# Latent attention in uniform 1024-column steps over three rotating PSUM pairs

## Chip, cores, metric

One Trainium2 chip, all 8 cores, one launch. The time is device microseconds of the slowest core. Such a program has a second, slower state in some executions, in which the cores of a die show a lower granted clock (the share of full TensorE speed that the profile records); those runs are marked slow and only fast runs are compared.

## The reference, cut to what matters

```python
# 8 heads, rank-compressed q and kv; block-causal over 64-frame chunks
q  = (rms_norm(c_q,  g_q)  @ w_uq ).reshape(B, S, 8, 128 + 64)    # nope | rope
kv = (rms_norm(c_kv, g_kv) @ w_ukv).reshape(B, S, 8, 128 + 128)   # k_nope | v
s = (einsum('bqhd,bkhd->bhqk', q_nope, k_nope) + einsum('bqhd,bkd->bhqk', q_pe, k_pe)) * scale
p = softmax(where(k_chunk <= q_chunk, s, NEG))
y_mla = einsum('bhqk,bkhd->bqhd', p, v) * silu(z_mla)
# ... sliding-window and memory groups, output projection, residual, final norm
```

Each core owns 1024 queries of one batch and sees all 4096 keys. The mask is a part of the rotary operand (64 extra rows), so it needs no instruction of its own.

## The kernel before: the parts concerned

Scores stand transposed, keys on partitions and queries on columns. PSUM has 8 banks: 0 to 3 are two pairs for scores, 4 and 5 the outputs of the two query halves, 6 the softmax sums, 7 the single bank in which the next head's operands (Q, rotary Q, K, V) are built. DVE takes its instructions in program order: the prediction shows a cast that starts at 580.10 behind two adds, although its matmuls were done before 578.9.

```python
def rec_s(n):                       # one step: two key tiles, 512 - c0 queries
    ... 4 score matmuls into pair n % 2
    act(AF.Exp, pb[:, :, c0:512], DB[k][:, c0:512], ...)
    if pr == 1:                     # add four tiles to one, for the sums
        tt(ALU.add, q2, pa, pb);  tt(ALU.add, q4, q2[:, 0], q2[:, 1])

def rec_pv(n):
    ... 2 PV matmuls into bank 4 + half
    if pr == 1:
        matmul(bank 6, lhsT=ones, rhs=q4)            # inline sum
        if last:                                     # close a half
            act(AF.Ln, rim, bank 6); act(AF.Exp, rim, rim, scale=-1.0)
            tt(ALU.mult, tmm, bank 4 + half, rim);  tt(ALU.mult, gate, tmm, gate)

for n in range(len(steps)):         # 24 steps per head, widths 512 / 384 / 256 / 128
    rec_s(n)
    if n >= 2: rec_pv(n - 2)
    if gen_next: gen_next.pop(0)()  # one of 20 operand jobs, 512 columns, always in bank 7
```

A job is its matmuls and one evacuation, the copy from PSUM to SBUF: K by an ACT copy, V and Q by a DVE cast, rotary Q by two DVE multiplies and an add.

The softmax here doesn't subtract the row's maximum and nothing guards it: scores larger than these inputs give would overflow.

Of the kernel before, what the change touches and what calls it, by code (L numbers as in the profile page):

```python
# [6 lines left out]
F32 = mybir.dt.float32  # L7
BF16 = mybir.dt.bfloat16
# [6 lines left out]
KB = 1024  # L15
# [151 lines left out]
def build():  # L167
# [33 lines left out]
    def pf(b, c0, c1, p0=0, p1=128):  # L201
        o = (b % 2) * 512
        return DB[b // 2][p0:p1, o + c0:o + c1]
# [4 lines left out]
    def tt(op, out, a, b, reads, writes, eng="dve"):  # L208
        P.op(eng, lambda e: e.tensor_tensor(out=out, in0=a, in1=b, op=op), reads=reads, writes=writes)  # L209
# [5 lines left out]
    def cp(eng, out, in_, reads, writes):  # L215
        if eng == "act":
            act(AF.Copy, out, in_, reads, writes)
        else:
            P.op(eng, lambda e: e.tensor_copy(out=out, in_=in_), reads=reads, writes=writes)  # L219
# [552 lines left out]
    Qn = [P.sb("Qn", [128, 1024], BF16, (26 + 2 * i) * KB) for i in range(2)]  # L772
    Qp = [P.sb("Qp", [128, 1024], BF16, (30 + 2 * i) * KB) for i in range(2)]
    csq = P.sb("csq", [128, 1024], F32, 98 * KB)
    tq = P.sb("tq", [64, 2, 512], F32, 102 * KB)
    pm4 = [P.sb("pm4", [128, 2, 512], BF16, (106 + 2 * i) * KB) for i in range(4)]
    p2 = [P.sb("p2", [128, 2, 512], BF16, (150 + 2 * i) * KB) for i in range(2)]
    p4 = [P.sb("p4", [128, 512], BF16, (154 + i) * KB) for i in range(2)]
    rim = P.sb("rim", [128, 512], F32, 156 * KB)
    tmm = P.sb("tmm", [128, 512], F32, 158 * KB)  # L780
    P.dma("sp", csq.t[:], csq_d[:, :], csq, writes=[csq])
    for i in range(2):
        P.dma("pool", Qp[i].t[64:128, :], gtm_d[:, :], Qp[i], writes=[Qp[i]])
# [3 lines left out]
        P.dma("pool", wo[i].t[:].rearrange("p a b -> p (a b)"), wo_d[i], wo[i], writes=[wo[i]])  # L787
    kpeT.w = kpeT.w + oh_ev

    def gen(h, banks):  # L790
        s = h % 2
        K_, V_, Qn_, Qp_ = Kb[s], Vb[s], Qn[s], Qp[s]
        ch = []

        def qn(half, gb):
            hs = slice(half * 512, (half + 1) * 512)

            def mm(e):
                for kc in range(4):
                    ins = e.matmul(pf(gb, 0, 512), lhsT=wuq.t[:, kc, h * 256:h * 256 + 128], rhs=cqT.t[:, kc, hs],  # L800
                                   start=(kc == 0), stop=(kc == 3))
                return ins
            P.op("pe", mm, reads=[wuq, cqT], writes=[PS[gb]])
            cp("dve", Qn_.t[:, hs], pf(gb, 0, 512), [PS[gb]], [Qn_])

        def qp(half, gb):
            hs = slice(half * 512, (half + 1) * 512)

            def mm(e):
                for kc in range(4):  # L810
                    ins = e.matmul(pf(gb, 0, 512), lhsT=wuq.t[:, kc, h * 256 + 128:h * 256 + 256], rhs=cqT.t[:, kc, hs],
                                   start=(kc == 0), stop=(kc == 3))
                return ins
            P.op("pe", mm, reads=[wuq, cqT], writes=[PS[gb]])
            tt(ALU.mult, tq.t[:, 0, :], pf(gb, 0, 512, 0, 64), csq.t[0:64, hs], [PS[gb], csq], [tq])
            tt(ALU.mult, tq.t[:, 1, :], pf(gb, 0, 512, 64, 128), csq.t[64:128, hs], [PS[gb], csq], [tq])
            tt(ALU.add, Qp_.t[0:64, hs], tq.t[:, 0, :], tq.t[:, 1, :], [tq], [Qp_])
            Qp_.w = Qp_.w + mask_ev[s]

        def kg(c8, gb):  # L820
            def mm(e):
                for kc in range(2):
                    ins = e.matmul(pf(gb, 0, 512), lhsT=wukv.t[:, kc, h * 256:h * 256 + 128],  # L823
                                   rhs=kvnT.t[:, kc, c8 * 512:(c8 + 1) * 512], start=(kc == 0), stop=(kc == 1))
                return ins
            P.op("pe", mm, reads=[wukv, kvnT], writes=[PS[gb]])
            cp("act", K_.t[:, c8 * 512:(c8 + 1) * 512], pf(gb, 0, 512), [PS[gb]], [K_])

        def vg(c8, gb):
            def mm(e):  # L830
                for t4 in range(4):
                    tl = c8 * 4 + t4
                    for kc in range(2):
                        ins = e.matmul(pf(gb, t4 * 128, (t4 + 1) * 128), lhsT=kvnT.t[:, kc, tl * 128:(tl + 1) * 128],  # L834
                                       rhs=wukv.t[:, kc, h * 256 + 128:h * 256 + 256], start=(kc == 0), stop=(kc == 1))
                return ins
            P.op("pe", mm, reads=[wukv, kvnT], writes=[PS[gb]])
            cp("dve", V_.t[:, c8 * 4:(c8 + 1) * 4, :].rearrange("p a b -> p (a b)"), pf(gb, 0, 512), [PS[gb]], [V_])

        for half in range(2):  # L840
            ch.append((qn, half))
            ch.append((qp, half))
        for c8 in range(8):
            ch.append((kg, c8))
            ch.append((vg, c8))
        return [(lambda f=f, a=a, gb=banks[i % len(banks)]: f(a, gb)) for i, (f, a) in enumerate(ch)]

    for c in gen(0, list(range(8))):
        c()


    steps = []
    for h in range(8):
        for half in range(2):
            kgs = list(range(4 * half + 4))
            for kg_ in kgs:
                c0 = max(0, kg_ - 4 * half) * 128
                for pr in range(2):
                    tiles = [kg_, 8 + kg_] if pr == 0 else [16 + 2 * kg_, 17 + 2 * kg_]
                    steps.append((h, half, kg_, c0, pr, tiles, kg_ == 0, kg_ == kgs[-1]))  # L860
    SKEW = 1
    pendq = []
    gen_next = []
    cur_h = -1

    def rec_s(n):
        h, half, kg_, c0, pr, tiles, first, last = steps[n]
        s, k, pb = h % 2, n % 2, pm4[n % 4]

        def mm(e):  # L870
            for t in range(2):
                kc = slice(tiles[t] * 128, (tiles[t] + 1) * 128)
                qs = slice(half * 512 + c0, half * 512 + 512)
                e.matmul(pf(2 * k + t, c0, 512), lhsT=Kb[s].t[:, kc], rhs=Qn[s].t[:, qs], start=True, stop=False)  # L874
                ins = e.matmul(pf(2 * k + t, c0, 512), lhsT=kpeT.t[:, kc], rhs=Qp[s].t[:, qs], start=False, stop=True)  # L875
            return ins
        P.op("pe", mm, reads=[Kb[s], Qn[s], Qp[s], kpeT], writes=[PS[2 * k], PS[2 * k + 1]])
        act(AF.Exp, pb.t[:, :, c0:512], DB[k][:, :].rearrange("p (a b) -> p a b", b=512)[:, :, c0:512],
            [PS[2 * k], PS[2 * k + 1]], [pb], scale=MLA_SCALE)
        if pr == 1:  # L880
            pa = pm4[(n - 1) % 4]
            q2, q4 = p2[(n // 2) % 2], p4[(n // 2) % 2]
            tt(ALU.add, q2.t[:, :, c0:512], pa.t[:, :, c0:512], pb.t[:, :, c0:512], [pa, pb], [q2])
            tt(ALU.add, q4.t[:, c0:512], q2.t[:, 0, c0:512], q2.t[:, 1, c0:512], [q2], [q4])

    def rec_pv(n):
        h, half, kg_, c0, pr, tiles, first, last = steps[n]
        s, pb = h % 2, pm4[n % 4]
        ob, lb = 4 + half, 6
        q4 = p4[(n // 2) % 2]  # L890

        def mm(e):
            for t in range(2):
                ins = e.matmul(pf(ob, c0, 512), lhsT=Vb[s].t[:, tiles[t], :], rhs=pb.t[:, t, c0:512],  # L894
                               start=(first and pr == 0 and t == 0), stop=(last and pr == 1 and t == 1))
            return ins
        P.op("pe", mm, reads=[Vb[s], pb], writes=[PS[ob]])
        if pr == 1:
            P.op("pe", lambda e: e.matmul(pf(lb, c0, 512), lhsT=ones.t[:], rhs=q4.t[:, c0:512], start=first, stop=last),
                 reads=[q4, ones], writes=[PS[lb]])  # L900
            if last:
                hs = slice(half * 512, (half + 1) * 512)
                act(AF.Ln, rim.t[:], pf(lb, 0, 512), [PS[lb]], [rim])
                act(AF.Exp, rim.t[:], rim.t[:], [rim], [rim], scale=-1.0)
                tt(ALU.mult, tmm.t[:], pf(ob, 0, 512), rim.t[:], [PS[ob], rim], [tmm])
                tt(ALU.mult, gate.t[:, h, hs], tmm.t[:], gate.t[:, h, hs], [tmm, gatep[h][half]], [gatep[h][half]])

    xo = [None] * 8

# [1 line left out]
        xo[i] = P.sb("xo", [128, D], F32, off * KB)  # L911
        P.dma("sp", xo[i].t[:], xo_d[i], xo[i], writes=[xo[i]])

    for n in range(len(steps)):
        h = steps[n][0]
        if h != cur_h:
            cur_h = h
            gen_next = gen(h + 1, [7]) if h < 7 else []
        rec_s(n)
        if n >= 2:  # L920
            rec_pv(n - 2)
        if gen_next:
            gen_next.pop(0)()
        if h == 7 and n % 24 == 3:
            for i, off in enumerate((34, 126)):
                wo.append(P.sb("wo", [128, 16, 512], BF16, off * KB))
                P.dma("pool", wo[2 + i].t[:].rearrange("p a b -> p (a b)"), wo_d[2 + i], wo[2 + i], writes=[wo[2 + i]])
            for i, off in enumerate((2, 10, 114, 142)):
                load_xo(i, off)
    rec_pv(len(steps) - 2)  # L930
    rec_pv(len(steps) - 1)


    gfin = P.sb("gfin", [128, D], F32, 198 * KB)
# [173 lines left out]
```

## Time and profile before

| | before |
|---|---|
| fast runs | 1003.8, 1004.4, 1004.8 us |
| slow run | 1108.7 us |
| until the first operand job (core 0) | 474.0 us |
| head 0's operands | 14.4 us |
| attention stage: first scores to first projection matmul | 389.2 us |
| output projection to the end | 125.5 us |
| a head with jobs / head 7 | 51.3 / 29.1 us |

The last five rows are cut from core 0's timeline; the first four of these add up to its span of 1003.1 us. Here and below the attention stage begins with the first rotary score matmul, 0.2 us after the very first score, where the prediction begins it (so it has 14.2 for head 0's operands). The lines that carry this are shown in the prediction. DVE of the kernel before, in order of time, around the 3.27 us hole:

```profile
543.84 0.69 DVE L209 TENSOR_TENSOR tmm_137<-psd,rim_136 128x512 f32<-128x512 f32 x1
544.63 0.69 DVE L209 TENSOR_TENSOR gate_103<-tmm_137,gate_103 128x512 bf16<-128x512 f32 x1
545.24 1.47 DVE L209 TENSOR_TENSOR tq_127<-psd,csq_126 64x512 f32<-64x512 f32 x2
```

The rotary evacuation (`tq`) that PE waits for until 546.86 stands behind the two multiplies that close the previous half (`tmm`, `gate`), and these need two ACT operations on the sums. Here the two were done by 543.74 and cost nothing more, because two adds held DVE from 542.63 to 543.85: in front of this cast stand both, adds and multiplies.

### The profile page before, as it was taken

The numbers are of one execution on the slowest core, as the hardware profiler recorded it, in microseconds if no ns is written. First come the engines' busy times: TensorE is split into PE (matmuls) and PEld (weight loads), VectorE is DVE, ScalarE is ACT, GpSimd is POOL, SyncE is SP. The second block draws the span as 40 slices with busy tenths as digits, with TensorE's granted clock in tenths as the row PEclk, the third lists the DMA queues.
The fourth block names the chain that finished last, engine by engine and source line by source line (L and its number), as shares of the span: only waits on it lengthen the run. The fifth ranks groups of instructions, "written<-read, shape, count | busy, mean of one in ns | idle before, by whom it ended". The sixth has DMA issues, their size and how long they took to land.

```text
span 1003.1 us, 12701 instructions; the slowest of 8 cores (987.9 to 1003.1 us)
## 1 busy us (share of the span) xinstructions
PE 811.1 (81%) x4461; PEld 394.0 (39%) x4540; DVE 520.4 (52%) x750; ACT 433.4 (43%) x593; POOL 16.3 (2%) x32
## 2 busy tenths in 40 slices
PE   0687987695999899899777777777777878999995
PEld 0244543243454333344433344443444434434442
DVE  0456654575665587677734444444444443424333
ACT  1336556311014467546354554545454536712221
POOL 2010000000000000000000000000000000000000
PEclk9889998899899999899999999999999989999998
DMA  9999538342563223876400000000000002991222
GB/s 171 233 170 171 98 52 150 156 163 89 205 257 127 85 103 108 157 200 140 81 1 1 1 1 1 2 0 1 1 1 1 2 1 66 211 289 64 85 85 84
DMA packets 18466, 95.55 MB, mean 95 GB/s; under 512 B 1826, under 2 KB 6050, under 8 KB 9380
## 3 DMA queue, kind: packets, MB, share of 16 engines
q0 software_dynamic: 7168, 30.15, 18.7%
q1 hardware_dynamic: 11236, 64.59, 18.2%
q8 instruction: 37, 0.61, 0.3%
q14 instruction: 25, 0.20, 0.1%
HBM read 116.49 MB, written 8.39 MB: 124 GB/s over the span
## 4 chain that ended last, share of the span: by engine, by line
PE 53%; DVE 15%; DMA 11%; ACT 11%; issue 9%; DVEq 0%; SPq 0%; ACTq 0%; POOL 0%; POOLq 0%
PE psd L562 14%; PE psd L947 10%; PE psd L327 9%; DMA wo_141<-wo 4%; PE psd L875 4%; PE psd L874 3%; PE psd L823 3%; ACT pm_87_129 L206 3%; DMA hown_57<-xu 2%; DVE tq_127 L209 2%; DMA wst_76<-wkv 2%; DMA stage_85<-wti 2%; DVE p_90_132 L209 2%; PE psd L894 2%; DVE Vb_121 L219 2%
## 5 line engine op out<-in xcount | busy, mean ns | idle before, releaser
L823 PE MATMUL psd<-kvnT_53,wukv_117 128*128 128x512 bf16 x120 | 36.6, 381 | 57.0 <-DVE Vb_121 L219 27.5
L209 DVE TENSOR_TENSOR p_90_132<-pm_86_128,pm_87_129 128x1024 bf16<-128x1024 bf16 (+1 forms) x48 | 29.0, 603 | 90.6 <-ACT pm_87_129 L206 90.4
L562 PE MATMUL psd<-hown_57,ring_86 128*128 128x512 bf16 x280 | 69.7, 408 | 6.1 <-DVE kmT_93 L209 4.8
L209 DVE TENSOR_TENSOR p_91_133<-pm_88_130,pm_89_131 128x768 bf16<-128x768 bf16 (+2 forms) x48 | 24.7, 514 | 84.8 <-ACT pm_89_131 L206 84.8
L206 ACT ACTIVATE pm_86_128<-psd 128x1024 bf16<-128x1024 f32 (+1 forms) x48 | 42.3, 882 | 59.7 <-PE psd L875 23.4
L562 PE MATMUL psd<-hown_57,ring_88 128*128 128x512 bf16 x281 | 63.8, 379 | 4.3 <-DVE zrt_113 L209 2.1
L875 PE MATMUL psd<-Qp_125,kpeT_54 128*128 128x512 bf16 (+3 forms) x192 | 61.5, 334 | 1.0 <-issue 0.4
L875 PE MATMUL psd<-Qp_124,kpeT_54 128*128 128x512 bf16 (+3 forms) x192 | 61.5, 334 | 1.0 <-issue 0.4
L874 PE MATMUL psd<-Qn_122,Kb_118 128*128 128x512 bf16 (+3 forms) x184 | 57.9, 329 | 0.7 <-ACT Kb_118 L206 0.7
L874 PE MATMUL psd<-Qn_123,Kb_119 128*128 128x512 bf16 (+3 forms) x184 | 57.8, 328 | 0.5 <-ACT pm_86_128 L206 0.4
L327 PE MATMUL psd<-hown_57,wkv_63 128*128 128x512 bf16 x125 | 34.6, 440 | 26.1 <-DMA hown_57<-xu 25.9
L206 ACT ACTIVATE pm_89_131<-psd 128x768 bf16<-128x768 f32 (+2 forms) x48 | 35.4, 738 | 39.6 <-PE psd L875 38.8
L562 PEld LDWEIGHTS psd<-hown_57,ring_86 128*128 128x128 bf16 x288 | 29.4, 104 | 44.8 <-issue 16.8
L206 ACT ACTIVATE pm_87_129<-psd 128x1024 bf16<-128x1024 f32 (+1 forms) x48 | 42.3, 881 | 10.0 <-PE psd L875 8.9
L834 PE MATMUL psd<-wukv_117,kvnT_53 128*128 128x128 bf16 x512 | 41.2, 226 | 4.1 <-ACT Kb_119 L206 1.2
L206 ACT ACTIVATE pm_88_130<-psd 128x768 bf16<-128x768 f32 (+2 forms) x48 | 35.2, 734 | 20.9 <-PE psd L875 15.6
L562 PEld LDWEIGHTS psd<-hown_57,ring_88 128*128 128x128 bf16 x288 | 27.5, 98 | 38.5 <-issue 6.6
L834 PEld LDWEIGHTS psd<-wukv_117,kvnT_53 128*128 128x128 bf16 x512 | 34.4, 101 | 20.8 <-issue 12.5
L823 PEld LDWEIGHTS psd<-kvnT_53,wukv_117 128*128 128x128 bf16 x128 | 8.8, 96 | 76.2 <-issue 75.2
L800 PE MATMUL psd<-cqT_92,wuq_116 128*128 128x512 bf16 x64 | 18.1, 409 | 22.6 <-DVE tq_127 L209 21.7
L562 PE MATMUL psd<-hown_57,ring_89 128*128 128x512 bf16 x158 | 35.8, 379 | 0.1
L562 PE MATMUL psd<-hown_57,ring_87 128*128 128x512 bf16 x155 | 35.5, 379 | 0.3
(308 smaller groups left out, 1537.1 us busy)
## 6 DMA issues: line engine op xcount, KB each, us to landing
stage_84<-wti SPq DMA_DIRECT2D x18, 1024.0 KB, 5.0
stage_85<-wti SPq DMA_DIRECT2D x10, 1024.0 KB, 5.3
stage_85<-wmk SPq DMA_DIRECT2D x8, 1024.0 KB, 5.8
hown_57<-xu POOLq DMA_DIRECT2D x4, 1024.0 KB, 28.7
wst_76<-wkv SPq DMA_DIRECT2D x2, 1024.0 KB, 14.6
hrot_58<-xu POOLq DMA_DIRECT2D x2, 1024.0 KB, 23.3
hrot_59<-xu POOLq DMA_DIRECT2D x2, 1024.0 KB, 28.8
hrot_60<-xu POOLq DMA_DIRECT2D x2, 1024.0 KB, 29.1
```

The source lines that it names most:

```text
L206: P.op("act", lambda e: e.activation(out=out, in_=in_, func=func, **kw), reads=reads, writes=writes)
L209: P.op(eng, lambda e: e.tensor_tensor(out=out, in0=a, in1=b, op=op), reads=reads, writes=writes)
L219: P.op(eng, lambda e: e.tensor_copy(out=out, in_=in_), reads=reads, writes=writes)
L327: ins = e.matmul(pf(b, 0, 512), lhsT=wkv.t[:, kc, g * 128:(g + 1) * 128], rhs=hpart(u, kc), start=(kc == 0), stop=(kc == 15))
L562: ins = e.matmul(pf(b, 0, 512), lhsT=wb.t[:, kc, :], rhs=hown.t[:, kc, hf * 512:(hf + 1) * 512], start=(kc == 0), stop=(kc == 15))
L800: ins = e.matmul(pf(gb, 0, 512), lhsT=wuq.t[:, kc, h * 256:h * 256 + 128], rhs=cqT.t[:, kc, hs], start=(kc == 0), stop=(kc == 3))
L823: ins = e.matmul(pf(gb, 0, 512), lhsT=wukv.t[:, kc, h * 256:h * 256 + 128], rhs=kvnT.t[:, kc, c8 * 512:(c8 + 1) * 512], start=(kc == 0), s ...
L834: ins = e.matmul(pf(gb, t4 * 128, (t4 + 1) * 128), lhsT=kvnT.t[:, kc, tl * 128:(tl + 1) * 128], rhs=wukv.t[:, kc, h * 256 + 128:h * 256 + ...
L874: e.matmul(pf(2 * k + t, c0, 512), lhsT=Kb[s].t[:, kc], rhs=Qn[s].t[:, qs], start=True, stop=False)
L875: ins = e.matmul(pf(2 * k + t, c0, 512), lhsT=kpeT.t[:, kc], rhs=Qp[s].t[:, qs], start=False, stop=True)
L894: ins = e.matmul(pf(ob, c0, 512), lhsT=Vb[s].t[:, tiles[t], :], rhs=pb.t[:, t, c0:512], start=(first and pr == 0 and t == 0), stop=(last a ...
L947: ins = e.matmul(pf(b, 0, 512), lhsT=gate.t[:, kc, tt_ * 128:(tt_ + 1) * 128], rhs=wo[ci].t[:, kc, :], start=(kc == 0), stop=(kc == 15))
```

## The change

Intent: keep PE free of waits by (1) 18 steps per head, all 1024 columns wide, by packing the diagonal's 384+128 and 256+256 columns into full banks; (2) ten double-width operand jobs that share three rotating PSUM pairs with the scores; (3) adds two steps later; (4) sums collected at the end of a half. Core of the diff, condensed:

```diff
-    tq = P.sb("tq", [64, 2, 512], F32, 102 * KB)
-    pm4 = ... 4 buffers;  p4 = ... 2 buffers
+    tq = [P.sb("tq", [64, 1024], F32, o * KB) for o in (102, 202)]
+    pmb = ... 6 buffers;  p4 = ... 12 buffers
+    def slot():
+        slot_i[0] += 1
+        k = slot_i[0] % 3
+        return k, [PS[2 * k], PS[2 * k + 1]]
     ...
+            for g in range(base + 1):
+                grp.append([[[(ti(g, o)[t], 0, 512, 0)] for t in range(2)] for o in range(2)])
+            grp.append([[[(ti(base + 1, o)[t], 128, 512, 128), (ti(base + 3, o)[t], 0, 128, 384)] ...
+            grp.append([[[(ti(base + 2, 0)[t], 0, 256, 256), (ti(base + 2, 1)[t], 256, 512, 256)] ...
     ...
+    def front(n):   # scores into slot(), one Exp over 1024 columns; no adds here
+    def back(n):    # PV; then, at the end of a group, the two adds into q2, q4
+    def close(h, hf):
+        k, ps = slot()
+        ... all sums of the half in one run of matmuls; Ln, Exp, tmm, gate as before
     ...
-        rec_s(n); if n >= 2: rec_pv(n - 2); if gen_next: gen_next.pop(0)()
+        front(n)
+        if gq and (i * 10) // (per_head - 1) + len(gq) > 9: gq.pop(0)()
+        back(n - 2)
+        ... close(h, hf) two steps after a half's last PV
```

Outputs are in banks 6 and 7. Head 0's operands use the same three pairs, where they had all eight banks.

## The prediction

> **What bounds the kernel now.** The diff touches only the latent-attention stage, so I first located that stage and asked how busy each engine is in it. The page's first section gives the whole span, and the table by stretches cuts core 0 (the slowest) at my own marks: building head 0's operands, heads 0 to 6, one typical head, and head 7 (columns: stretch, length, busy PE, PEld, DVE, ACT, POOL, granted clock, DMA share, GB/s).
>
> ```profile
> PE 811.1 (81%) x4461; PEld 394.0 (39%) x4540; DVE 520.4 (52%) x750; ACT 433.4 (43%) x593; POOL 16.3 (2%) x32
> ```
>
> ```profile
> 473.90:488.10 14.20, 11.12 (x94) 6.53 (x96) 12.57 (x20) 6.67 (x11) 0.26 (x1) 1.00 0.94 170
> 488.10:848.20 360.10, 275.47 (x1731) 145.49 (x1760) 165.94 (x306) 179.89 (x250) 0.00 (x0) 0.96 0.01 1
> 591.60:642.90 51.30, 38.97 (x249) 20.82 (x252) 23.89 (x45) 25.82 (x36) 0.00 (x0) 0.97 0.00 1
> 848.20:877.30 29.10, 27.22 (x159) 14.17 (x161) 13.98 (x30) 20.93 (x28) 1.06 (x2) 1.00 1.03 233
> ```
>
> A head that also builds the next head's operands takes 51.3 us, with PE busy for 39 and DVE and ACT for 24 and 26. Nobody is full, so the head is bound by waiting. Head 7 builds nothing and takes 29.1. Next, what PE waits for between 488.1 and 877.3 us (the chain of waits, PE only, longest first):
>
> ```profile
> PE psd L823 <- DVE Vb_121 L219: 27.5, 22, 2.5
> PE psd L800 <- DVE tq_127 L209: 21.7, 7, 3.5
> PE psd L823 <- DVE Vb_120 L219: 19.6, 15, 2.8
> PE psd L823 <- DVE tq_127 L209: 8.7, 7, 1.3
> ```
>
> L800 and L823 are the operand jobs. These four lines are 77.5 us of PE waiting, all for DVE to empty the one bank (7) that all jobs share. Why DVE is late shows in the timeline of one pair of steps, engine by engine (PE, then ACT, then DVE):
>
> ```profile
> 576.28 0.59 PE L823 MATMUL psd<-kvnT_53,wukv_117 128*128 128x512 bf16 x2 [0.80 <-DVE Vb_120 L219]
> ...
> 578.23 0.61 PE L834 MATMUL psd<-wukv_117,kvnT_53 128*128 128x128 bf16 x8
> ...
> 580.93 0.59 PE L823 MATMUL psd<-kvnT_53,wukv_117 128*128 128x512 bf16 x2 [0.80 <-DVE Vb_120 L219]
> ```
>
> ```profile
> 577.84 1.02 ACT L206 ACTIVATE pm_89_131<-psd 128x1024 bf16<-128x1024 f32 x1 [0.27 <-PE psd L875]
> ```
>
> ```profile
> 578.96 0.69 DVE L209 TENSOR_TENSOR p_91_133<-pm_88_130,pm_89_131 128x1024 bf16<-128x1024 bf16 x1 [2.83 <-ACT pm_89_131 L206]
> 579.76 0.42 DVE L209 TENSOR_TENSOR p_93_135<-p_91_133 128x512 bf16<-128x512 bf16 x1
> 580.10 0.68 DVE L219 CAST Vb_120<-psd 128x512 bf16<-128x512 f32 x1
> ```
>
> The V job's matmuls (578.23) are done before 578.9, but in DVE's program order its cast stands behind two adds that need the exponential of the same step (577.84 to 578.86). The cast ends at 580.78, and only then may the K job at 580.93 write bank 7. The period of such a pair is 580.93 - 576.28 = 4.65 us.
>
> **A second cost of the gaps.** Around a Q job:
>
> ```profile
> 543.00 0.59 PE L894 MATMUL psd<-pm_86_128,Vb_121 128*128 128x512 bf16 x2
> 546.86 1.87 PE L800 MATMUL psd<-cqT_92,wuq_116 128*128 128x512 bf16 x4 [3.27 <-DVE tq_127 L209]
> 548.52 0.53 PE L874 MATMUL psd<-Qn_123,Kb_119 128*128 128x384 bf16 x1
> ```
>
> After the 3.27 us hole four 512-column matmuls take 548.52 - 546.86 = 1.66 us, 0.415 each. Elsewhere they start 0.216 us apart. That is the granted clock of 0.93 to 0.97 in heads 0 to 6, against 1.00 in head 7. Over 360 us a clock of 0.96 loses up to 14 us.
>
> **What the Trainium skill says.**
> - "TensorE: Matmul & The Clock Gate", "What's actually happening": after an idle window of about 3.4 us the array runs at half rate until it has been busy for about as long. The trace agrees: 0.415 against 0.216 us after a hole of 3.27 us.
> - "Perfetto Trace Analysis", "Matmuls": independent matmul groups should rotate through different PSUM banks, so that emptying one overlaps the next group. Bank 7 is the opposite, and the 77.5 us above agree.
> - "ScalarE: Activation LUTs", "What ACT_TABLE_LOAD costs": an ACTIVATE with immediate scale and bias takes 186 ns + 0.833 ns per element. That gives 1039 and 612 ns for 1024 and 512; the trace has 1024 and 596. One 1024-wide copy is therefore cheaper than two of 512.
> - "VectorE: DVE Perf Modes", "The perf-mode tier table": bf16 `tensor_tensor` in SBUF runs at 2x, and fp32 operands from PSUM lose that. The trace agrees: a 1024-wide bf16 add takes 0.69 us, a 512-wide cast out of PSUM 0.68.
>
> **The change, part by part, per head.**
>
> *PE work stays equal.* Scores: half 0 has key-group widths 512+384+256+128 = 1280 columns, half 1 has 4x512 more, 3328. Together 4608, times 4 tiles, times 3 (nope and rope scores, PV), plus 4608 for the sums: 59,904 columns. The new steps pack 384+128 and 256+256 into one 512-wide bank, so the columns are the same, in 18 steps instead of 24. The operand jobs are 3 x 8192 = 24,576 columns. Eight heads of attention and seven of jobs are 651,264 columns. At 0.216 us per 512 that is 274.8 us. The trace shows 128-column score matmuls spaced at 0.055 us, so narrow pieces cost nothing extra. The stage now takes 877.3 - 488.1 = 389.2 us, so 114 us are waits and half clock. This is the most that the loop can give.
>
> *What is removed.* (1) Bank 7 goes: ten double jobs take turns with the scores in three pairs. (2) The adds move from the step itself to two steps later, behind the cast, so no cast waits for an exponential any more. (3) The sums move to the end of a half, so PE never waits for them inside a step.
>
> *What may wait afterwards.* A step is 4 score matmuls (0.86 us) and 2 PV (0.43); a K or V job is about 0.88, a Q job 1.73. A pair comes round after three allocations: between the end of a job and the reuse of its pair lie at least PV, scores, PV, scores = 2.57 us. Freeing it takes about 0.3 us until the evacuation starts (gaps in the timeline above), 1.22 us for a 1024-wide DVE op out of PSUM (the trace has such ops at L212, 1.22) and about 0.15 us back: 1.7. The rotary Q job needs two such ops: 2.9, so a wait of some 0.3 us unless a close lies between. Exponentials: 0.3 + 1.02 + 0.15 = 1.5 us against at least 2.1. I book 1 to 1.5 us of waits per head, 10 us in all, and 1 us at the end (last adds before the last sums).
>
> *Engine totals after.* ACT: 18 exponentials x 1.02 + 4 K copies x 1.02 + 2 closes x (0.59 + 0.63) = 25 us. DVE: casts 5 x 1.22, rotary 3 x 1.22, adds 8 x (0.69 + 0.42) + 2 x (0.42 + 0.29), closes 4 x 0.69 = 23 us. PE: 35.6 us. Both helpers stay below 70% of PE. With no hole above 1 us the half-clock stretches should go too.
>
> *Head 0's operands.* 14.2 us now, DVE-bound behind the last gates (busy 12.6). DVE's own part is 3 x 1.22 + 5 x 1.22 = 9.8 us instead of about 10.8: 1 us less.
>
> *The end.* In the output projection:
>
> ```profile
> 877.57 3.40 PE L947 MATMUL psd<-wo_138,gate_103 128*128 128x512 bf16 x15 [0.20 <-issue]
> ...
> 890.03 5.30 PE L947 MATMUL psd<-wo_141,gate_103 128*128 128x512 bf16 x15 [2.15 <-DMA wo_141<-wo]
> ```
>
> The fourth weight block starts loading at 851.6, once head 6's last PV frees the buffer, and needs 38 us. In the new order that read is again the second step of head 7, about 26 us before the projection, as now (851.1 to 877.3). So this stall of 2.2 us stays; the residual loads issued just before it start some 1.5 us later relative to it, so I book 1 us more. Head 7's own gain is thus hidden under the transfer.
>
> *Sum.* 389.2 - (274.8 + 10 + 1) = 103.4 us saved, plus 1, less 1: 1004.4 - 103 = 901. I say 902.
>
> **Rivals.**
> - *The shared pairs become the new wait.* All evacuations and exponentials now release the same three pairs, and one late evacuation stalls scores, not only a job. For: the rotary job's 2.9 against 2.6 us, and DVE being in order behind the closing multiplies, which wait for two ACT ops. Against: DVE is at 64% of PE. At 0.5 us for each of 70 jobs it adds 35 us: about 930.
> - *The clock drops as PE gets denser.* [...]Against: the projection after 895 us runs dense on all cores at 0.216 us per matmul. If 0.96 stayed, 11 us more: 913.
> - *The gain is hidden by the weight load.* If head 7 shortens more than I think, the stall at 890 grows by as much. It touches only head 7's few us: at most 4 us, 906.
> - *No new wait and the loop at its floor:* 1004.4 - 114 - 1 = 889.
>
> **Range and chances.** The floor sets the low end, 889. The high end allows the pair waits at half of the first rival together with part of the clock: 922. The gaps are over 100 us wide and their single cause is removed, so faster by over 2% (under 984) is nearly sure: 0.97; within 2% 0.02, slower 0.01.
>
> **What would show it.** Right: a head period of 36.5 to 38 us; the waits of L800 and L823 for DVE gone, with no single PE wait line above about 5 us; granted clock 0.99 or more through the stage; PE busy near 1.0 of full slices; head 7 to projection about unchanged, with a stall on the fourth weight block of 2 to 4 us. Wrong: score matmuls waiting for casts or exponentials in every step (first rival), matmuls spaced well above 0.216 us without a hole before them (second), or a stall at the projection above 5 us (third).

## The result

Fast runs 894.7, 894.7 and 895.3 us, one slow run 980.3. The ratio to before is 0.891, 95% interval 0.889 to 0.893 (a ratio is the mean time of one kernel's fast runs over that of the other's of the same rounds, so not quite the ratio of the medians). 902 was predicted, with a range of 889 to 922.

Core 2 is the slowest after the change, so here is the same core in both:

| core 2, us | before | after |
|---|---|---|
| until the first operand job | 474.6 | 472.3 |
| head 0's operands | 14.4 | 17.6 |
| attention stage | 388.4 | 278.2 |
| projection to the end | 123.8 | 125.2 |
| span | 1001.1 | 893.2 |

The attention stage is 278.2 us on all eight cores. By the prediction's count its floor is 274.8.

The page's first section, kernel after:

```profile
PE 789.7 (88%) x4540; PEld 395.0 (44%) x4540; DVE 505.6 (57%) x654; ACT 420.2 (47%) x513; POOL 16.3 (2%) x32
```

PE is busy for 21 us less, although its columns are the same. The matmuls at half clock are gone, which by my estimate is up to 14 us of it (0.96 of full clock over 360 us before, 1.00 now); the rest is not itemised. The same table by stretches as before (heads 0 to 6, then one head):

```profile
489.60:739.30 249.70, 249.41 (x1749) 144.11 (x1749) 150.31 (x218) 167.11 (x180) 0.00 (x0) 1.00 0.00 1
...
596.60:632.50 35.90, 35.90 (x253) 20.79 (x252) 21.92 (x32) 24.15 (x26) 0.00 (x0) 1.00 0.01 1
```

PE is busy for all of a head, at a granted clock of 1.00, and a head takes 35.9 us instead of 51.3. DVE (21.9 us per head) and ACT (24.2) come out about 1 us below the prediction's 23 and 25. What PE waits for, from just before the first scores into the projection:

```profile
PE psd L992 <- DMA wo_154<-wo: 3.0, 1, 3.0
PE psd L889 <- ACT Kb_118 L206: 0.7, 1, 0.7
PE psd L903 <- ACT pmb_134 L206: 0.4, 1, 0.4
PE psd L931 <- DVE p_104_146 L209: 0.3, 1, 0.3
PE psd L834 <- DVE tq_128 L209: 0.3, 1, 0.3
```

Where before 77.5 us stood in four lines, the last three lines, 1.0 us in all, are the listed waits of the stage. (The first line is the projection's, and the second, 0.7 us, ends with the first score.) DVE's order, kernel after:

```profile
562.50 1.22 DVE L219 CAST Qn_123<-psd 128x1024 bf16<-128x1024 f32 x1 [1.98 <-PE psd L810]
563.64 0.68 DVE L209 TENSOR_TENSOR p_93_135<-pmb_132,pmb_133 128x1024 bf16<-128x1024 bf16 x1
```

The cast now waits for nothing but its own matmuls, and the adds follow it.

Two stretches got longer. Head 0's operands (PE, kernel after):

```profile
478.28 1.05 PE L848 MATMUL psd<-wukv_117,kvnT_53 128*128 128x128 bf16 x16 [1.52 <-DVE Qn_122 L219]
480.73 1.87 PE L834 MATMUL psd<-kvnT_53,wukv_117 128*128 128x512 bf16 x4 [1.40 <-DVE tq_128 L209]
```

With three pairs, job 4 waits for the pair of job 1, and job 5 for that of job 2, while DVE is only just through with the last multiplies of the stage before (the gates, until 477.0). After the two holes four matmuls take 1.87 instead of 1.03 us on this core; on cores 0, 1 and 3, with the same two holes, they take 1.02, and their operands 15.7 us. About 1 us of the longer time is an earlier start: before, the first job waited 0.94 us for a bank that DVE was still reading, and now it begins with another pair. And the stall on the fourth weight block (first line of the waits) is 3.0 us on this core, where the kernel before has 1.9.

### The profile page after: what moved, and what is told of

It reads as the page before. It is cut to its first block, busy times and chain, and to the rows that moved or that the text cites. A ratio compares the mean times of both kernels' runs of the same rounds, so it can differ in the third digit from the quotient of the medians.

```text
span 893.2 us, 12300 instructions; the slowest of 8 cores (883.7 to 893.2 us)
## 1 busy us (share of the span) xinstructions
PE 789.7 (88%) x4540; PEld 395.0 (44%) x4540; DVE 505.6 (57%) x654; ACT 420.2 (47%) x513; POOL 16.3 (2%) x32
## 3 DMA queue, kind: packets, MB, share of 16 engines
q1 hardware_dynamic: 11236, 64.59, 21.6%
## 4 chain that ended last, share of the span: by engine, by line
PE 68%; DMA 15%; DVE 7%; ACT 5%; issue 4%; SPq 0%; DVEq 0%; POOL 0%; ACTq 0%; POOLq 0%
PE psd L562 15%; PE psd L992 11%; PE psd L327 8%; PE psd L890 6%; PE psd L889 6%; PE psd L903 6%; DMA wo_154<-wo 4%; DMA stage_84<-wti 4%; PE psd L834 3%; PE psd L848 3%; PE psd L810 3%; DMA hown_57<-xu 3%; DMA wst_76<-wkv 2%; PE psd L931 1%; DMA hrot_58<-xu 1%
## 5 line engine op out<-in xcount | busy, mean ns | idle before, releaser
L562 PE MATMUL psd<-hown_57,ring_86 128*128 128x512 bf16 x288 | 70.8, 407 | 4.2 <-DVE ring_86 L209 4.2
L562 PE MATMUL psd<-hown_57,ring_88 128*128 128x512 bf16 x288 | 64.5, 379 | 4.3 <-DVE zrt_113 L209 2.9
L889 PE MATMUL psd<-Qn_122,Kb_118 128*128 128x512 bf16 (+2 forms) x192 | 59.5, 326 | 0.7 <-ACT Kb_118 L206 0.7
L889 PE MATMUL psd<-Qn_123,Kb_119 128*128 128x512 bf16 (+2 forms) x192 | 59.5, 326 | 0.0
L890 PE MATMUL psd<-Qp_125,kpeT_54 128*128 128x512 bf16 (+2 forms) x192 | 57.9, 326 | 0.0
L890 PE MATMUL psd<-Qp_124,kpeT_54 128*128 128x512 bf16 (+2 forms) x192 | 57.8, 326 | 0.0
L327 PE MATMUL psd<-hown_57,wkv_63 128*128 128x512 bf16 x128 | 34.0, 430 | 25.8 <-DMA hown_57<-xu 25.8
L562 PEld LDWEIGHTS psd<-hown_57,ring_86 128*128 128x128 bf16 x288 | 29.3, 104 | 44.5 <-issue 16.5
L562 PEld LDWEIGHTS psd<-hown_57,ring_88 128*128 128x128 bf16 x288 | 27.5, 98 | 39.1 <-issue 7.2
L206 ACT ACTIVATE pmb_130<-psd 128x1024 bf16<-128x1024 f32 x24 | 24.6, 1023 | 31.2 <-PE psd L890 9.9
L848 PE MATMUL psd<-wukv_117,kvnT_53 128*128 128x128 bf16 x512 | 35.0, 223 | 1.5 <-DVE Qn_122 L219 1.5
L562 PE MATMUL psd<-hown_57,ring_89 128*128 128x512 bf16 x160 | 36.0, 380 | 0.2 <-DVE zrt_112 L209 0.2
L834 PE MATMUL psd<-kvnT_53,wukv_117 128*128 128x512 bf16 x128 | 34.6, 394 | 1.7 <-DVE tq_128 L209 1.7
L562 PE MATMUL psd<-hown_57,ring_87 128*128 128x512 bf16 x160 | 35.9, 380 | 0.0
L848 PEld LDWEIGHTS psd<-wukv_117,kvnT_53 128*128 128x128 bf16 x512 | 32.1, 100 | 8.3 <-issue 3.1
L219 DVE CAST Vb_121<-psd 128x1024 bf16<-128x1024 f32 x16 | 19.6, 1224 | 26.5 <-PE psd L848 26.5
L327 PEld LDWEIGHTS psd<-hown_57,wkv_63 128*128 128x128 bf16 x128 | 13.9, 109 | 45.1 <-issue 34.2
L219 DVE CAST Vb_120<-psd 128x1024 bf16<-128x1024 f32 x16 | 19.6, 1224 | 23.0 <-PE psd L848 23.0
L206 ACT ACTIVATE pmb_132<-psd 128x1024 bf16<-128x1024 f32 x24 | 24.4, 1017 | 16.7 <-DVE tq_127 L209 12.4
L992 PE MATMUL psd<-wo_154,gate_103 128*128 128x512 bf16 x128 | 28.9, 379 | 3.0 <-DMA wo_154<-wo 3.0
L316 PE MATMUL psd<-qt_66,ones_43 128*128 128x512 bf16 x32 | 11.6, 500 | 22.1 <-DVE r2t_71 L212 16.6
L810 PE MATMUL psd<-cqT_92,wuq_116 128*128 128x512 bf16 x128 | 30.1, 379 | 0.0
```

The source lines that it names most:

```text
L206: P.op("act", lambda e: e.activation(out=out, in_=in_, func=func, **kw), reads=reads, writes=writes)
L219: P.op(eng, lambda e: e.tensor_copy(out=out, in_=in_), reads=reads, writes=writes)
L316: ins = e.matmul(pf(6, 0, 512), lhsT=ones.t[:], rhs=qt.t[:, c, :], start=(c == 0), stop=(c == 3))
L327: ins = e.matmul(pf(b, 0, 512), lhsT=wkv.t[:, kc, g * 128:(g + 1) * 128], rhs=hpart(u, kc), start=(kc == 0), stop=(kc == 15))
L562: ins = e.matmul(pf(b, 0, 512), lhsT=wb.t[:, kc, :], rhs=hown.t[:, kc, hf * 512:(hf + 1) * 512], start=(kc == 0), stop=(kc == 15))
L810: ins = e.matmul(pf(2 * k + hf, 0, 512), lhsT=wuq.t[:, kc, col:col + 128], rhs=cqT.t[:, kc, hf * 512:(hf + 1) * 512], start=(kc == 0), sto ...
```

## The experiments

Totals are of fast runs. "Stage" is the attention stage in the trace; unless a spread is given, it is the same on all cores within 0.8 us, including cores whose clock was low in other stages.

| kernel | total, us | stage, us | over the floor of 274.8 |
|---|---|---|---|
| before | 1004.4 | 388.4 (385.3 to 392.9) | 114 |
| old + adds after the job | 976.5 | 365.5 (363.5 to 366.9) | 91 |
| old + adds + late closing multiplies | (disturbed) | 316.8 | 42 |
| old + two job banks | 921.5, 923.3 | 309.0 | 34 |
| old + all three | (disturbed) | 316.9 | 42 |
| new, two pairs, inline sums | 1047.6 (disturbed) | 412.4 to 415.2 | 138 to 140 |
| new, two pairs | 924.0 | 307.8 | 33 |
| new, diagonal not merged | 904.4 | 289.5 | 15 |
| new, adds ahead of the cast | 899.1, 901.6, 904.4 | 287.1 | 12 |
| **new (the change)** | 894.7 | 278.2 | 3 |

The theory to test was the prediction's: the casts were late because adds stood in front of them, and the shared bank did the rest. Rivals: the number of banks alone, or the uniform steps alone. The double width of the jobs has no run of its own.

### 1. Old kernel, adds behind the job

```diff
         rec_s(n)              # the two adds taken out into rec_add
         if n >= 2: rec_pv(n - 2)
         if gen_next: gen_next.pop(0)()
+        rec_add(n)
```

> The kernel before with one thing moved: the two adds of a step are issued to DVE after that step's operand job, so the cast that frees bank 7 no longer stands behind adds that need the same step's exponential. One bank, 24 steps and inline sums stay. Theory 'order' (the casts were late only because of what stood in front of them): the 77 us of PE waits at L800/L823 fall to 20-35 us (rotary Q jobs and narrow diagonal steps, which give a single bank too little time), head period 40 to 41.5 us instead of 51.3, time 925 to 940 us. Theory 'banks' (one bank shared by all jobs is the limit whatever the order): head period above 48 us, time above 985 us. Theory 'steps' (narrow uneven steps are the limit): the same, above 985 us.

Measured: 976.5 us, ratio 0.975 (0.973 to 0.977), stage 23 us shorter. Between both theories. In wide steps it does what was said: a pair of steps takes 3.68 us (K jobs at 563.77 and 567.45) instead of 4.65. But the long waits stay (PE, whole stage):

```profile
PE psd L823 <- DVE Vb L219: 21.6, 15, 2.8
PE psd L800 <- DVE tq L209: 20.3, 7, 3.3
PE psd L903 <- DVE p L209: 10.2, 17, 2.6
```

DVE of this kernel shows what makes them:

```profile
557.86 0.69 DVE L209 TENSOR_TENSOR tmm<-psd,rim 128x512 f32<-128x512 f32 x1 [3.50 <-ACT rim L206]
558.65 0.69 DVE L209 TENSOR_TENSOR gate<-tmm,gate 128x512 bf16<-128x512 f32 x1
559.26 0.68 DVE L219 CAST Vb<-psd 128x512 bf16<-128x512 f32 x1
```

The V cast is behind the closing multiplies, which wait for ACT. The seven waits of the Q jobs (20.3 us in the list) and those of some 2.5 us of K jobs look like this one; experiment 2 tests it. The third line of the waits (L903, the inline sum) has grown: the adds now stand behind the cast, and the sums wait for them (the kernel before had 3.2 us in its two lines of this kind).

### 2. Closing multiplies one step later as well

```diff
             if last:
                 act(AF.Ln, ...); act(AF.Exp, ...)
-                tt(ALU.mult, tmm, ...);  tt(ALU.mult, gate, ...)
+                late_mul.append((n + 3, h, half, ob))
     ...
         rec_add(n)
+        rec_mul(n)                  # the two multiplies, when their step has come
```

> The reordered old kernel (adds after the job) with a second thing moved: the two multiplies that close a half are issued to DVE one step later, behind the next job's cast, instead of ahead of it. In the reordered kernel alone PE still had two holes per head, 3.3 us at L800 and 2.5 us at L823, each with the closing multiplies ahead of the cast on DVE. Theory 'close' (those multiplies, which wait for two ACT ops, make these holes and the half-clock stretch after them): both holes fall below 1 us, 35 to 45 us less than the 977 of adds alone: 930 to 942 us. Rival 'one bank is too little around the Q jobs anyway': above 965 us.

The chip was disturbed: four runs between 943 and 1022 us, with six cores at a granted clock of 0.94 even in the profiled run, so the total says nothing. The stage is clear: 316.8 us, 49 less than with the adds alone, a little more than the 35 to 45 expected, at a granted clock of 1.00 over the stage of every core (0.96 to 0.97 with the adds alone). The two long lines of waits, 20.3 and 21.6 us, have shrunk to these (PE, core 2):

```profile
PE psd L800 <- DVE tq L209: 4.6, 7, 0.7
PE psd L823 <- DVE Vb L219: 0.3, 1, 0.3
```

So in this order of repair the closing multiplies, with the half clock after their holes, were worth twice the adds. They were not moved alone, so how the two share the 72 us is not shown.

### 3. Old kernel in its old order, two job banks

```diff
-        ob, lb = 4 + half, 6
+        ob, lb = 4 + half, 5 - half         # sums in the idle output bank
-            gen_next = gen(h + 1, [7])
+            gen_next = gen(h + 1, [6, 7])
```

> The kernel before, in its old order, with two banks for the operand jobs instead of one (the sums use the idle one of the two output banks). Theory 'banks': a late cast then has a whole further step before its bank is wanted, so the waits for adds vanish and the two close holes per head shrink by about 1.8 us each: 930 to 950 us. Theory 'order' alone: the casts stay late, time above 975 us.

Measured: 921.5 and 923.3 us, ratio 0.920 (0.915 to 0.924), stage 309.0. (The verdict on record is unclear; only two runs of each kernel were fast.) What PE still waits for at the job banks (core 5):

```profile
PE psd L811 <- DVE tq L209: 6.0, 6, 1.2
PE psd L834 <- DVE tq L209: 4.9, 7, 0.8
PE psd L834 <- DVE Vb L219: 4.4, 14, 0.7
```

The theory 'banks' held and gained more than it had said. So two repairs that share nothing, the better order with one bank (experiment 2) or one more bank with the old order, each take away some 70 to 80 of the 114 us. Most of the loss needed both, the bad order and the single bank.

### 4. All three on the old kernel

The diffs of 1, 2 and 3 together.

> All three on the kernel before: adds after the job, closing multiplies a step later, two job banks. The 24 uneven steps of 512-wide banks, two score pairs, inline sums and the single-width jobs stay. Theory 'release of the job banks is the whole cause': PE waits below 20 us in all, head period 36.5 to 38 us, 900 to 915 us, so the uniform steps, merged diagonals and double jobs would be worth less than 15 us. Rival 'the uniform 1024-column steps matter in their own right': above 925 us.

A miss. The chip was disturbed (943 us and more; the cores that kept their clock in the profiled run, 0, 1, 4 and 5, took 916 to 928), but the stage, 316.9 us, is no shorter than with order alone and longer than with banks alone; 900 to 915 us would have needed less than 300. Where PE waits (core 5, which kept its clock):

```profile
PE psd L903 <- DVE p L209: 17.1, 25, 1.5
PE psd L903 <- DVE tmm L209: 10.6, 6, 2.1
```

L903 is the inline sum. Every wait at a job's bank is gone, and the time went to the sums: they wait for adds that now stand behind casts, and for their bank, which the late closing multiplies still hold. 27.7 of the 42 us over the floor are in these two lines. The rest I have not itemised.

### 5. Changed kernel with two pairs, and the sums inline again

```diff
-        k = slot_i[0] % 3
+        k = slot_i[0] % 2
```

> The changed kernel with two PSUM pairs in rotation instead of three (the third unused). By the arithmetic of the prediction a pair then comes back after two allocations, about 1.3 us where a job stands between: 0.2 us of wait for scores behind an exponential (1.5), 0.4 for a job behind a cast (1.7), 1.6 behind the rotary Q job (2.9): some 7 us per head, head period 42 to 44, time 935 to 955 us. If the order of DVE's work is all that matters: time below 905 us.

Measured: 924.0 us, ratio 0.923 (0.921 to 0.925), stage 307.8. The third pair is worth 30 us of stage; I had expected 40 to 60, and 935 to 955 us. The waits that the profile lists sum to some 17 us; it does not itemise the small ones that make up the rest.

With two pairs, banks 4 and 5 are free, and the deferred sums can be undone:

```diff
     # back(n), behind the two adds of a group:
-        lsum.setdefault(key, []).append((q4, cols))
+        P.op("pe", ms, reads=[ones, q4], writes=[PS[4 + st["hf"]]])   # the sum, here
```

> The changed kernel with two rotating pairs, and in the two banks so freed the sums inline again: each group's sum right behind its PV on PE, as before the change, instead of at the end of the half. To be compared with the two-pair kernel, whose attention stage took 307.8 us. Putting the adds late and giving the jobs two banks left 42 us over the floor in the old kernel, 25 of them PE waiting at the sums for adds and closing multiplies. Theory 'late adds need deferred sums' : PE waits at the sums for adds that stand behind a cast, in some five groups per head by 1 to 2 us: stage 325 to 370 us. Rival 'where the sums stand costs nothing': within 3 us of 307.8.

Stage 412.4 to 415.2 us: some 105 us more than with two pairs and deferred sums, and longer than the kernel before. It was profiled once, on a disturbed chip. PE's longest wait (core 0, 488 to 880 us) and the DVE work in front of one such sum:

```profile
PE psd L923 <- DVE p L209: 88.8, 40, 3.7
```

```profile
545.78 1.23 DVE L219 CAST Vb<-psd 128x1024 bf16<-128x1024 f32 x1 [4.78 <-PE psd L848]
546.92 0.68 DVE L209 TENSOR_TENSOR p<-pmb,pmb 128x1024 bf16<-128x1024 bf16 x1
547.71 0.43 DVE L209 TENSOR_TENSOR p<-p 128x512 bf16<-128x512 bf16 x1
...
548.28 0.38 PE L923 MATMUL psd<-p,ones 128*128 128x512 bf16 x1 [2.17 <-DVE p L209]
```

A double-wide cast goes first, then two adds, then the sum, with PE idle for 2.2 us. So with two pairs the late adds, and each sum right behind them, make the stage longer than before the change. In the kernel before, a sum stood two steps behind its adds. That distance was not tried with the late adds of the new kernel (in the old one, with adds behind the job, it left the 17.1 us of experiment 4). So it is shown that a sum cannot stand right behind late adds, but not that it must wait for the end of the half.

### 6. Changed kernel, adds back ahead of the cast

```diff
     # front(n), behind the Exp (moved from back(n)):
+        if not st["gend"]: return
+        tt(ALU.add, q2, pa, pb);  tt(ALU.add, q4, q2[:, 0], q2[:, 1])
```

> The changed kernel with the adds put back where they were: in the step itself, on DVE ahead of the operand job's cast. Three pairs, double jobs, merged steps and deferred sums stay. Theory 'order' (needed even with three pairs): a V or Q cast ends about 3.2 us after its job where the pair is wanted 2.6 us after it, so 0.5 to 1 us of wait on about half of the jobs, head period 38 to 40 us, time 910 to 925 us. Theory 'banks' (three pairs cover the late cast): head period 36 to 36.5, time within 3 us of 895.

Measured: 899.1 to 904.4 us, ratio 0.902 (0.898 to 0.905), stage 287.1. Between the two theories (910 to 925, or within 3 us of 895): the order still matters, but with three pairs only 9 us of stage. Once there are three pairs, the late adds are a small part of the gain.

### 7. Changed kernel, diagonal not merged

```diff
-            for g in range(base + 1): ...          # full groups
-            grp.append(... 384 + 128 ...);  grp.append(... 256 + 256 ...)
+            for g in range(base + 4):
+                c_ = max(0, g - base) * 128
+                grp.append([[[(ti(g, o)[t], c_, 512, c_)] for t in range(2)] for o in range(2)])
```

> The changed kernel with the diagonal tiles not merged: 24 steps per head, the last three key groups of a half narrow as before; everything else of the change stays. PE columns are equal. Theory 'merging is a detail': narrow steps give short reuse times, about 0.2 to 0.5 us of wait in some of the 12 narrow steps, head period 36.5 to 38 us, time 898 to 910 us. Rival 'uniform steps are what removes the waits': head period above 40 us, time above 925 us.

Measured: 904.4 us (903.4 to 907.0), ratio 0.903 (0.901 to 0.906), stage 289.5: as 'merging is a detail' expected. It is worth 11 us of stage.

### 8. Two repairs of what got longer

The changed kernel was run again as the yardstick for the next three, on the same chip.

> The changed kernel unaltered, as the yardstick for the three that follow on the same chip: 895 us within 0.5%, attention stage (first scores of head 0 to first matmul of the output projection) 278.1 us, head 0's operands 15.7 to 17.6 us by core, a stall of 3 us on the fourth weight block of the projection on the slowest core.

Fast runs 896.4 and 898.3 us, two slow; stage 278.2; operands 15.7 to 17.7.

Head 0's operands over four pairs:

```diff
-        k = slot_i[0] % 3
+        k = slot_i[0] % nslot[0]       # 4 while head 0's operands are built, then 3
```

> The changed kernel, but head 0's operand jobs, which run before any scores, rotate through four PSUM pairs (the output pair is idle then); afterwards three as before. In the changed kernel head 0's operands take 15.7 to 17.6 us against 14.4 before, with PE waiting for casts of the pair three jobs back and a half-clock stretch after it. If the three pairs are the cause: 13.5 to 14.5 us, time 1.5 to 3 us less than the changed kernel. Rival (DVE, busy with the last gates until 4.6 us into the stage, is the limit whatever the pairs): within 0.5 us of the changed kernel.

Operands 15.8 to 16.6 us, against 15.7 to 17.7 for the yardstick: the 13.5 to 14.5 that the theory 'pairs' asked for did not come. But the edit made a wait of its own (PE, core 2, the first score):

```profile
478.94 0.38 PE L890 MATMUL psd<-Qn,Kb 128*128 128x512 bf16 x1 [1.69 <-DVE Vb L219]
```

After ten jobs over four pairs, the count over three gives the first scores the very pair that the last V job has just filled, so they wait for its cast. The changed kernel waits 0.7 us at this place, for a K copy. By this difference, an estimate of mine, the fourth pair saved about 1 us more than it shows, and the run does not decide between pairs and DVE. The total, 891.2 to 893.7 us, lies 3 to 7 us under the yardstick's two fast runs. The stages do not account for that, so I count it as inconclusive.

The fourth weight block first, during head 6:

```diff
+            if i == 5 and steps[n]["h"] == 6:
+                wo3 = P.sb("wo", [128, 16, 512], BF16, 126 * KB)
+                P.dma("pool", wo3..., wo_d[3], wo3, writes=[wo3])
             if i == 4 and steps[n]["h"] == 7:
-                ... both blocks
+                ... the third block only; wo.append(wo3)
```

> The changed kernel, but the fourth weight block of the output projection is loaded first and already in head 6, as soon as the last Q job has freed its room; the third as before. If the 3 us stall at the projection is only the late start of that transfer: the stall goes, 2.5 to 4 us less than the changed kernel, about 892. Rival (the stall moves to the third block or to the residual loads, which share the same transfer time): within 1 us of 895.

Fast runs 888.1, 890.1 and 890.5 us, ratio to before 0.887 (0.884 to 0.890). The stall is gone on all eight cores, and the projection to the end takes 122.0 to 122.2 us on every core (in a profiled run that was slow, but at a clock of 1.00 from the attention stage on), where the yardstick has 122.7 to 126.5. That is up to 4.4 us, on core 7, whose stall was 2.6 us and was followed by 3.4 us at half clock. It agrees with the theory. Of the 7.7 us between the means of the fast runs, the rest lies outside this stage.

Both, with two of head 0's V casts on ACT:

> Both of these, and two of head 0's four V casts on ACT, which is idle there. Expected: head 0's operands 12 to 13.5 us, no stall at the projection, 5 to 8 us less than the changed kernel: 887 to 890 us. If the gains do not add (the slowest core is set by something earlier): above 892.

Fast runs 889.9 and 890.6 us: no better than the early weight block alone. Operands 15.0 to 16.7 us. A miss against 12 to 13.5: PE still waits 0.63 and 1.43 us for the evacuations of the Q jobs, which come after the gates, and again for the last V job's pair, 1.76 us, as in the run with four pairs. The best version is therefore the change with the early weight block, 889.6 us in the mean of its three fast runs, 0.9% under the yardstick on the same chip (897.3) and 0.6% under the changed kernel's first runs on another (894.9). All its fast runs are below all fast runs of both kernels.

## Why the prediction was right, and where its steps failed

1. **The floor.** 651,264 columns at 0.216 us per 512 gave 274.8 us, and the stage measured 278.2. The central step held. Of the 3.4 us on top 1.0 are listed waits; the rest is not itemised. The number needs only that all waits go, not why they stood there, so it came out right although the next step was wrong.
2. **"Their single cause is removed."** This is the step that failed as reasoning. I put all 77.5 us down to casts behind adds. Experiment 1 gave 23 us of stage for the adds alone, experiment 2 another 49 when the closing multiplies were moved too. The profile before has them in the timeline at 543.84, one view away from the hole that I had quoted and read only for its half clock. And experiment 3 shows that a second bank takes away 79 of the 110 us with no order touched. Bad order and single bank were one cause in two halves.
3. **Deferred sums** were a side remark ("PE never waits for them inside a step"). In experiment 5 the late adds cost 105 us of stage with two pairs when each sum stands right behind its adds.
4. **Waits booked, 10 us, and 1 at the end.** Measured 1.0 in the whole stage; a head took 35.9 us where 36.5 to 38 was said. The term was 0.3 us or more behind each rotary Q job (2.9 us to free a pair against 2.6). The trace has this wait once, 0.3 us, in head 0. In later heads the sums of the previous half (1.4 us of PE) come between, the "close" that the prediction mentioned but did not use. So the stage came out 7.6 us shorter than the 285.8 predicted. That the total missed by only 7 is in part luck: head 0 went the other way, by some 2 to 4 us (step 6).
5. **Clock.** Said: the half-clock stretches go, 0.99 or more. Measured: 1.00 in the stage. Right.
6. **Head 0's operands, 1 us less.** Wrong in sign: 14.4 (15.5 on core 1) became 15.7 to 17.6, about 1 us of it by the earlier start. The sum counted DVE's durations and forgot that PE cannot run ahead of DVE with three pairs instead of eight banks: PE waits 1.52 and 1.40 us for pairs, and then DVE waits for the matmuls of the V jobs (1.18, 1.66 and 0.53 us on core 2). How much a fourth pair mends stays open (experiment 8).
7. **The end, 1 us more.** Core 2's stall went from 1.9 to 3.0. Right: the fourth block's transfer takes 38.0 us in both kernels and starts 25.7 us before the projection in one, 24.7 in the other. Experiment 8 shows that an earlier start removes the stall.
8. **Rivals.** Shared pairs as the new wait: no, with three; yes, by 30 us, with two. Lower clock: no. Gain hidden by the weight load: the stall grew by 1.1 us on core 2, where this rival allowed 4.

Added up for core 2: 110.2 us from the stage, 2.3 from an earlier start (of which 0.94 is the wait of the first job for its bank, which the change removed; the rest lies before any changed line), less 3.2 for head 0 and 1.4 at the end, is 107.9, as much as its span fell.

## What to carry to other kernels

For each wait on a PSUM bank, list everything that stands in front of its evacuation on the in-order engine, and what that in turn waits for: here there were two different things, and in the order tested the rarer one was worth more. Name the causes of waits apart before you add the waits up, and try the cheap repair first: one more bank, two changed lines, gave 79 of 110 us. Moving work behind an evacuation delays whoever uses that work, so move the user back as well.

## What the Trainium skill lacked or had wrong

- "TensorE: Matmul & The Clock Gate", "Seeing it yourself": it advises to budget 1.95 GHz (13/16) for dense matmuls on all cores. In the fast runs here eight cores run the 278 us of dense attention at a granted clock of 1.00, 0.216 us per 512 columns. The page's figure does appear, but in another stage: in the profiled run with the early weight block, which was slow, core 4 was granted 0.81 from 203 to 239 and from 265 to 331 us, where core 0 had 0.99 to 1.00, and 1.00 again in its attention stage.
- The same page, "What's actually happening": it gives an idle window of about 3.4 us, and says that the windows run free of the kernel. Shorter holes were enough here, on some cores: after holes of 1.52 and 1.40 us with 1 us of work between, four matmuls took 1.43 to 1.87 us on cores 2 and 4 to 7, and 1.02 on cores 0, 1 and 3. After a hole of 2.17 us in the kernel with inline sums, matmuls were 0.43 us apart.
- "Perfetto Trace Analysis", "Matmuls": rotating banks is right (309.0 against 388.4 us of stage with a second bank), but the page does not say that the order of the evacuating engine can do nearly the same with one bank (316.8), nor that the two do not add (316.9).
- No page read here says what it costs when work is moved behind an evacuation and its user is not moved back: 105 us of stage with each sum left right behind its late adds.
